# Sliding-window attention: two key blocks folded into one before the exponential, GpSimd work in short pieces, and the gate projection moved between units

## The chip, the cores and the metric

The kernel runs on one core of a Trainium2 chip. The metric is the device time of one execution in microseconds, taken as the median of several runs. A profiled execution of the same program gives the trace from which the rows below are quoted; its span runs from the first to the last instruction. Engines are named as the profile does: PE is TensorE (matmuls), PEld its weight loads, DVE is VectorE, ACT is ScalarE, POOL is GpSimd, and SP is the engine whose queue issues the DMAs.

## The reference

The input is a sequence of 2048 rows of 1024 floats. Two layers follow each other. The first is a gated retention layer in chunks of 128 rows; its code is not touched here. The second is a gated sliding-window attention: 16 query heads of 64 columns share 2 key/value heads, keys are looked at in blocks of 128, and each query sees its own position and the 127 before it, so it needs its own key block and the one before. A sink per head enters the softmax's denominator.

```python
q, gate = jnp.split(rmsnorm(x, g_norm) @ w_in, [SWA_Q_WIDTH], axis=-1)
q = rmsnorm(q.reshape(b, nb, BLOCK, SWA_KV_HEADS, SWA_GROUP, SWA_HEAD_DIM), g_q)
scores = jnp.einsum('bnqkgd,bnjkd->bnkgqj', q, k_band) * (SWA_HEAD_DIM ** -0.5) + bias
scores = jnp.where(mask, scores, -jnp.inf)      # 0 <= dist < 128, key position >= 0
m = jnp.maximum(jnp.max(scores, axis=-1, keepdims=True), sink)
p = jnp.exp(scores - m)
p = p / (jnp.sum(p, axis=-1, keepdims=True) + jnp.exp(sink - m))
o = jnp.einsum('bnkgqj,bnjkd->bnqkgd', p, v_band).reshape(b, s, SWA_Q_WIDTH)
return x + (o * jax.nn.silu(gate)) @ w_out
```

Of the 256 keys of the two blocks exactly 128 are in a query's window: query i sees key j of its own block where j <= i, and key j of the block before where j > i. At any column j one of the two scores is therefore masked.

## The kernel before, in words

All arithmetic is fp32. A large matmul is split: each operand becomes a high part (type fp32r) and a low part, the difference, and three matmuls are summed (lines 149 to 151 and 153 to 155 in `proj`). The high part of a weight tile is made on ScalarE (L127) and the low part by a subtraction (L129), on VectorE in the retention layer and in the first pass over a weight, on GpSimd otherwise. A projection covers 512 rows, takes four PSUM banks, loads its weight in tiles of 128 x 1024 and yields after each tile and after its evacuation.

The attention layer is `phase_b`. Its unit is one group of 512 rows (4 of them) and one key/value head (2), 8 units in all. For a unit u there are:

- `main(u)`: for the first head of a group the keys and values (`evac_kv`, which fills the key store `kst` and the values `vst`), then the queries (`evac_q`: copy out of PSUM to `qn`, squares, sum, reciprocal root on GpSimd at L107/L108, scaling, split into `qs` at L804/L805, transposes at L813, copies to `qst` at L817 and L819).
- `gates(u)`: the gate projection; `evac_g` applies tanh (L833) and forms the gate (L834).
- `attn(u)`: for each of the four row blocks m and each parity `par` of the heads (a half, four heads): score matmuls over two key blocks (L870), addition of the bias and running minimum of the negated score into P (L873), the sink's term (L879, L880), the exponential with its sum (L881), denominator (L883, L884), scaling (L887), transposes of P by block (L891), copies to SBUF (L895 on VectorE, L897 on ScalarE). Then the product with V (L907), the gate (L910) and the split into `ohi` and `olo` (L911, L912).
- `out_b(u)`: the output projection of a unit's `ohi` and `olo`, whose evacuation adds the residual `res` (loaded and stored at L924 to L926). `ohi` and `olo` have one buffer each, so `out_b(u-1)` must have read them before `attn(u)` writes them.
- `prep_b(u)`: calls `prep`, which loads the rows of the next group, scales them (L189), and splits them (L191, L192) into `xhi` and `xlo`. `stats` makes the scale `rb` from row sums. `out_last` is the output projection of the last unit, in halves (L959 to L962).

`filler(u)` strings the projections that run beside `attn(u)`: gates of u, output projection of u-1, `main` of u+1. `drive` emits them in turns, one step of the filler for each 0.6 steps spent on attention (1.0 in the first unit), and gives attention's instructions a priority 300 places ahead; a planner with a model of times then sets the order on each engine. `attn(u)` does not emit a product with V before the gates of u are emitted.

Of the kernel before, what the change touches and what calls it, by code (L numbers as in the profile page):

```python
# [36 lines left out]
PSUM_BUFS = {"rr": 4, "s": 2, "f": 2}  # L37
RAW = 3
# [20 lines left out]
def tile_yoco(ctx, tc, x, x_t, w_qk, w_vg, wo_a, w_kv, w_b, wo_b, ag, kvg, bg, kng, qng,  # L59
# [53 lines left out]
    def wload(src, cols, name, kscale=None, key=None):  # L113
# [14 lines left out]
        eng = nc.gpsimd if psum["phase"] == "b" and kscale is None else nc.vector  # L128
        eng.tensor_tensor(lo, raw, hi.bitcast(F32), op=ALU.subtract)  # L129
        return hi, lo  # L130

    def proj(src, nk, xhi, xlo, feat, evac, name, kscale=None, key=None, cols=512, before=None):
        kn = 1024 // cols
        bk = [pbank("ab"[m // 2], f"pp_{name}_{m}") for m in range(4)]
        for kp in range(nk // kn):
            if before is not None:
                before(kp)
            hi, lo = wload(src[kp], cols, f"{name}_{kp}",
                           None if kscale is None else kscale[:, kp * kn : (kp + 1) * kn], (key, kp))
# [43 lines left out]
    def prep(g, rb):  # L183

        xhi, xlo = xt_tiles(f"b{g}")
        for kp in range(KT // 2):
            raw = wp.tile([P, 2, T], F32, tag="raw", bufs=RAW, name=f"xraw_b{g}_{kp}")
            nc.sync.dma_start(raw, xmid[g][kp])
            nc.gpsimd.tensor_tensor(raw, raw, rb.unsqueeze(1).to_broadcast([P, 2, T]), op=ALU.mult)  # L189
# [539 lines left out]
    def phase_b(pb):  # L729
# [4 lines left out]
        kst = cst.tile([P, KVH * 2, 2 * MT + 1, P], F32R, name="kst")  # L734
        gq = cst.tile([P, HD], F32, name="gq")
# [15 lines left out]
        def main(u):  # L751
            g, kv = units[u]
            n = f"b{u}"
            if kv == 0:
# [4 lines left out]
                vst = p2.tile([P, MT, KVH * HD], F32, tag="vst", name=f"vst_{n}")  # L759
                st["kv", g] = vst  # L760

                def evac_kv(m, ps):
                    kr = p1.tile([P, 512], F32, tag="qn", bufs=2, name=f"kn_{n}_{m}")
                    nc.scalar.copy(kr[:, : 2 * KVH * HD], ps[:, : 2 * KVH * HD])
                    nc.vector.tensor_copy(vst[:, m, :], kr[:, KVH * HD : 2 * KVH * HD])
# [21 lines left out]
                    nc.vector.tensor_copy(kst[:, :, kb + m + 1, :], tp.rearrange("p (a t) -> p a t", a=4))  # L787
# [5 lines left out]
            def evac_q(m, ps):  # L793
                qn = p1.tile([P, 512], F32, tag="qn", bufs=2, name=f"qn_{n}_{m}")
# [12 lines left out]
                qT = p1.tile([P, GQ, P], F32R, tag="qst", bufs=6, name=f"qst_{n}_{m}")  # L807
                qst.append(qT)
                for half in range(2):
# [6 lines left out]
                    if half:  # L816
                        nc.scalar.copy(dst, t3)  # L817
                    else:
                        nc.vector.tensor_copy(dst, t3)  # L819
# [4 lines left out]
        def gates(u):  # L824
# [10 lines left out]

            yield from proj(w_b[kv, 1], KT, xhi, xlo, True, evac_g, f"{n}g", kscale=bgs, key=("g", kv))
            st["gate", u] = gate

        def attn(u):
# [7 lines left out]
            for m in range(MT):  # L847
# [11 lines left out]
                for par in range(2):  # L859
# [3 lines left out]
                    for j in range(4):  # L863
# [5 lines left out]
                        for hl in range(2):  # L869
# [6 lines left out]
                            op0=ALU.add, op1=ALU.min, accum_out=nm[:, c : c + 1])  # L876
                        if j == 3:
# [3 lines left out]
                        nc.scalar.activation(pt[:, j, :w], pt[:, j, :w], AF.Exp, scale=-1.0,  # L881
                                             bias=nm[:, c : c + 1], accum_out=den[:, c : c + 1])
                    nc.vector.tensor_tensor(den[:, hs], den[:, hs], es[:, hs], op=ALU.add)  # L883
                    nc.vector.reciprocal(den[:, hs], den[:, hs])  # L884
                    for j in range(4):
                        c = 4 * par + j
                        nc.vector.tensor_scalar_mul(pt[:, j, :w], pt[:, j, :w], den[:, c : c + 1])  # L887
# [205 lines left out]
```

## Time and profile before

| | us |
|---|---|
| median of 3 runs | 2522.36 (2522.0 to 2522.67) |
| profiled execution, whole time | 2513.12 |
| its span | 2511.3 |
| TensorE busy / weight loads busy | 2446.6 / 1995.4 |
| VectorE, ScalarE, GpSimd busy | 1714.5, 1128.1, 477.2 |
| granted TensorE clock, mean | 0.99 |

Rows of groups read: line, engine, operation, output <- inputs, shape, count | busy time, mean ns of one | idle time of the engine ahead of them and what ended it. Rows of waits read: waiting instruction <- what ended the wait: total us, times, longest. Rows of stretches give the stretch, its length, busy us and instruction count of each engine, granted clock, share of the DMA engines, GB/s. Rows of tiles give shortest/median/longest ns. Matmuls are pipelined, so the duration of one is longer than the distance to the next.

### The profile page before, as it was taken

Reading aid. Unit: us, or ns where it says so; the run is one execution under the profiler, and the core shown is the slowest. Engines: PE = TensorE matmul, PEld = TensorE weight load, DVE = VectorE, ACT = ScalarE, POOL = GpSimd, SP = SyncE. Lnnn points to the kernel's source line nnn. Section 1 sums busy time; section 2 is a strip of 40 time slices with the busy share of each in tenths; the row PEclk is TensorE's granted clock in tenths of the full one; section 3 lists DMA queues with packets and bytes.
Section 4 is the critical chain, followed back from the end, with each engine's and each line's share of the span. In section 5 each row is a group of like instructions: output and inputs, shape, how many; then the busy total and the mean of one; then the engine's idle time right before and its main releaser. Section 6 shows DMA issues by size and latency. Waiting matters only on the chain.

```text
span 2511.3 us, 32377 instructions
## 1 busy us (share of the span) xinstructions
PE 2446.6 (97%) x11816; PEld 1995.4 (79%) x11816; DVE 1714.5 (68%) x2953; ACT 1128.1 (45%) x2008; POOL 477.2 (19%) x393
## 2 busy tenths in 40 slices
PE   8999999999999999999999999989899999999998
PEld 6888787888888888888888888777677777777887
DVE  5546674786868657667666576677867677677766
ACT  4333233544436445435354354435544455445553
POOL 0000000021000020000010000042335444353360
PEclk9999999999999999999999999999899999999999
DMA  8434873586636455465364243374233342342432
GB/s 294 135 115 132 262 268 119 162 290 228 229 119 201 147 168 159 158 212 184 119 206 152 91 159 111 103 256 156 76 118 122 105 156 74 132 144 84 135 116 94
DMA packets 141035, 395.05 MB, mean 157 GB/s; under 512 B 16411, under 2 KB 28876, under 8 KB 140876
## 3 DMA queue, kind: packets, MB, share of 16 engines
q1 hardware_dynamic: 140876, 392.99, 47.3%
q8 instruction: 93, 1.52, 0.2%
q14 instruction: 66, 0.54, 0.1%
HBM read 321.60 MB, written 74.47 MB: 158 GB/s over the span
## 4 chain that ended last, share of the span: by engine, by line
PE 81%; DMA 8%; DVE 7%; ACT 2%; issue 1%; POOL 0%; SPq 0%; DVEq 0%; ACTq 0%
PE pp_ao L151 4%; PE pp_ao L149 4%; PE pp_ao L150 4%; PE o_t L907 2%; PE s_t L870 2%; PE pT_t L891 2%; PE pp_bo L149 1%; PE pp_bo L150 1%; PE pp_bo L151 1%; DMA res<-xmid 1%; PE ot_r L643 1%; PE dl_r L607 1%; PE o_r L615 1%; PE dl_r L608 1%; PE o_r L617 1%
## 5 line engine op out<-in xcount | busy, mean ns | idle before, releaser
L149 PE MATMUL pp_ao<-ohi_r,whi_ao 128*128 128x512 f32 x512 | 199.7, 394 | 4.9 <-DVE x_r L679 2.7
L150 PE MATMUL pp_ao<-olo_r,whi_ao 128*128 128x512 f32 x512 | 201.7, 394 | 0.0
L107 POOL TENSOR_SCALAR r_o_r<-sso_r,ep 128x1 f32<-128x1 f32 x48 | 28.6, 596 | 904.6 <-ACT jo_r L637 904.6
L881 ACT ACTIVATE P_t<-P_t,nm_t 128x256 f32<-128x256 f32 (+1 forms) x256 | 127.7, 499 | 157.3 <-DVE nm_t L873 156.7
L151 PE MATMUL pp_ao<-ohi_r,wlo_ao 128*128 128x512 f32 x512 | 196.7, 394 | 0.1
L873 DVE CUSTOM_DVE_ANT_0 P_t<-s_t,bias,nsnk 128x256 f32<-128x256 f32 (+1 forms) x256 | 116.5, 470 | 36.8 <-PE s_t L870 35.8
L127 ACT CAST whi_ao<-raw_ao 128x1024 fp32r<-128x1024 f32 x64 | 67.2, 1050 | 153.1 <-issue 47.5
L129 DVE TENSOR_TENSOR wlo_ao<-raw_ao,whi_ao 128x1024 fp32r<-128x1024 f32 x64 | 78.1, 1223 | 81.7 <-ACT whi_ao L127 80.3
L703 ACT CAST Shi_r<-S 128x512 fp32r<-128x512 f32 x120 | 69.9, 618 | 116.5 <-PE o_r L617 88.0
L149 PEld LDWEIGHTS pp_ao<-ohi_r,whi_ao 128*128 128x128 f32 x512 | 96.9, 189 | 26.0 <-DVE x_r L679 3.1
L151 PEld LDWEIGHTS pp_ao<-ohi_r,wlo_ao 128*128 128x128 f32 x512 | 97.1, 190 | 21.7 <-DVE wlo_ao L129 1.1
L150 PEld LDWEIGHTS pp_ao<-olo_r,whi_ao 128*128 128x128 f32 x512 | 97.4, 190 | 20.5 <-issue 0.2
L704 DVE TENSOR_TENSOR Slo_r<-S,Shi_r 128x512 fp32r<-128x512 f32 x120 | 85.4, 737 | 40.1 <-ACT Shi_r L703 39.9
L870 PE MATMUL s_t<-kst,qst_b 128*128 128x256 f32 (+1 forms) x512 | 103.3, 299 | 8.6 <-DVE nm_t L873 8.5
L870 PEld LDWEIGHTS s_t<-kst,qst_b 128*128 128x128 f32 x512 | 84.8, 193 | 30.8 <-DVE nm_t L873 11.5
L630 DVE SCALAR_TENSOR_TENSOR S<-S,dl_r 128x512 f32<-128x512 f32 x112 | 74.6, 682 | 41.4 <-PE dl_r L609 41.3
L887 DVE TENSOR_SCALAR P_t<-P_t,den_t 128x256 f32<-128x256 f32 (+1 forms) x256 | 95.0, 434 | 1.8
L679 DVE TENSOR_TENSOR x_r<-x_r,pp_ao 128x512 f32<-128x512 f32 x128 | 84.0, 683 | 14.1 <-PE pp_ao L151 14.0
L149 PE MATMUL pp_bo<-ohi_t,whi_bo 128*128 128x512 f32 x224 | 89.1, 406 | 1.3 <-DVE gate_b L834 1.1
L150 PE MATMUL pp_bo<-olo_t,whi_bo 128*128 128x512 f32 x224 | 89.0, 397 | 0.0
L129 POOL TENSOR_TENSOR wlo_bo<-raw_bo,whi_bo 128x1024 fp32r<-128x1024 f32 x28 | 70.5, 2523 | 93.9 <-ACT whi_bo L127 80.0
L151 PE MATMUL pp_bo<-ohi_t,wlo_bo 128*128 128x512 f32 x224 | 87.7, 396 | 0.0
(1037 smaller groups left out, 7464.1 us busy)
## 6 DMA issues: line engine op xcount, KB each, us to landing
raw_ao<-in_wo_a SPq DMA_DIRECT2D x64, 512.0 KB, 3.6
b<-in_w_vg SPq DMA_DIRECT2D x64, 256.0 KB, 5.1
res<-xmid SPq DMA_DIRECT2D x56, 256.0 KB, 3.0
raw_bo<-in_wo_b SPq DMA_DIRECT2D x28, 512.0 KB, 3.6
x_r<-in_x_t SPq DMA_DIRECT2D x16, 512.0 KB, 5.8
xin<-in_x SPq DMA_DIRECT2D x16, 512.0 KB, 3.5
xmid<-x_r SPq DMA_DIRECT2D x16, 512.0 KB, 4.3
xraw_b<-xmid SPq DMA_DIRECT2D x16, 512.0 KB, 3.6
```

What stands on the lines that cost most here:

```text
L129: eng.tensor_tensor(lo, raw, hi.bitcast(F32), op=ALU.subtract)
L149: nc.tensor.matmul(o, hi[:, kk, sl], xh, start=st, stop=False)
L150: nc.tensor.matmul(o, hi[:, kk, sl], xl, start=False, stop=False)
L151: nc.tensor.matmul(o, lo[:, kk, sl], xh, start=False, stop=sp)
L630: nc.vector.scalar_tensor_tensor(S32[:, d, :], S32[:, d, :], gamC[h], dl[d], op0=ALU.mult, op1=ALU.add)
L679: nc.vector.tensor_tensor(t, t, ps, op=ALU.add)
L703: nc.scalar.copy(hi, src[:, d, :])
L704: nc.vector.tensor_tensor(lo, src[:, d, :], hi.bitcast(F32), op=ALU.subtract)
L870: nc.tensor.matmul(o, qst[m][:, h, :], kst[:, kv * 2 + hl, kb + b0 : kb + 2, :], start=hl == 0, stop=hl == 1)
L873: nc.vector.tensor_tensor_reduce(out=pt[:, j, :w], in0=o, in1=bias[:, kv * GQ + h, b0 * P :], scale=-1.0, scalar=nsv[:, h : h + 1], op0=AL ...
L881: nc.scalar.activation(pt[:, j, :w], pt[:, j, :w], AF.Exp, scale=-1.0, bias=nm[:, c : c + 1], accum_out=den[:, c : c + 1])
L887: nc.vector.tensor_scalar_mul(pt[:, j, :w], pt[:, j, :w], den[:, c : c + 1])
```

## The change

In attention the two key blocks of a half are folded by a minimum after every second head, so that P has 128 columns a head from there on. The exponential, the scaling (one instruction for four heads, with a broadcast) and the transposes run on these. The transposed P is copied twice, once as it is (ScalarE) and once times a triangular mask (VectorE). The first copy is multiplied with the values of the block before, the second with the difference of own values and those before, which `evac_kv` now makes beside the values. The first row block of the sequence has one key block and no fold.

GpSimd's subtractions for low parts are cut into pieces of 256 columns, the scaling in `prep` goes from GpSimd to VectorE, and copies to `qst` and `kst` go from VectorE to ScalarE. `qn` has four buffers for two, `qst` seven for six. In `filler`, the gates of unit u+1 follow `main(u+1)`, so they are emitted beside attention of u; those of the last unit stay at the start of the last filler. The row statistics come behind the output projection.

```diff
--- before.py
+++ after.py
@@ -35,6 +35,8 @@
 PSUM_BUFS = {"rr": 4, "s": 2, "f": 2}
+PIECE = 256
+QN = 4
 RAW = 3
@@ -125,8 +127,14 @@
         nc.scalar.copy(hi, raw)
-        eng = nc.gpsimd if psum["phase"] == "b" and kscale is None else nc.vector
-        eng.tensor_tensor(lo, raw, hi.bitcast(F32), op=ALU.subtract)
+        if psum["phase"] == "b" and kscale is None:
+            for k in range(kn):
+                for c in range(0, cols, PIECE):
+                    t = (slice(None), k, slice(c, c + PIECE))
+                    nc.gpsimd.tensor_tensor(lo[t], raw[t], hi[t].bitcast(F32), op=ALU.subtract)
+        else:
+            nc.vector.tensor_tensor(lo, raw, hi.bitcast(F32), op=ALU.subtract)
         return hi, lo
@@ -186,7 +195,7 @@
             nc.sync.dma_start(raw, xmid[g][kp])
-            nc.gpsimd.tensor_tensor(raw, raw, rb.unsqueeze(1).to_broadcast([P, 2, T]), op=ALU.mult)
+            nc.vector.tensor_tensor(raw, raw, rb.unsqueeze(1).to_broadcast([P, 2, T]), op=ALU.mult)
             hi, lo = xhi[kp], xlo[kp]
@@ -732,6 +741,8 @@
         kst = cst.tile([P, KVH * 2, 2 * MT + 1, P], F32R, name="kst")
+        mask = cst.tile([P, P], F32, name="mask_b")
+        nc.sync.dma_start(mask, mask_t)
         gq = cst.tile([P, HD], F32, name="gq")
@@ -756,13 +767,18 @@
                     nc.gpsimd.tensor_copy(kst[:, :, 0, :], kst[:, :, 2 * MT, :].bitcast(F32))
-                vst = p2.tile([P, MT, KVH * HD], F32, tag="vst", name=f"vst_{n}")
+                vst = p2.tile([P, 2, MT, KVH * HD], F32, tag="vst", name=f"vst_{n}")
                 st["kv", g] = vst
                 def evac_kv(m, ps):
-                    kr = p1.tile([P, 512], F32, tag="qn", bufs=2, name=f"kn_{n}_{m}")
+                    kr = p1.tile([P, 512], F32, tag="qn", bufs=QN, name=f"kn_{n}_{m}")
                     nc.scalar.copy(kr[:, : 2 * KVH * HD], ps[:, : 2 * KVH * HD])
-                    nc.vector.tensor_copy(vst[:, m, :], kr[:, KVH * HD : 2 * KVH * HD])
+                    v = vst[:, 0, m, :]
+                    nc.vector.tensor_copy(v, kr[:, KVH * HD : 2 * KVH * HD])
+                    if g or m:
+                        before = (vst if m else st["kv", g - 1])[:, 0, (m - 1) % MT, :]
+                        nc.vector.tensor_tensor(vst[:, 1, m, :], v, before, op=ALU.subtract)
                     kr = kr[:, : KVH * HD]
@@ -784,14 +800,14 @@
                         nc.tensor.transpose(tr[:, j * P : (j + 1) * P], kd[:, j // 2, j % 2, :], ident_r)
-                    nc.vector.tensor_copy(kst[:, :, kb + m + 1, :], tp.rearrange("p (a t) -> p a t", a=4))
+                    nc.scalar.copy(kst[:, :, kb + m + 1, :], tp.rearrange("p (a t) -> p a t", a=4))
...
             def evac_q(m, ps):
-                qn = p1.tile([P, 512], F32, tag="qn", bufs=2, name=f"qn_{n}_{m}")
+                qn = p1.tile([P, 512], F32, tag="qn", bufs=QN, name=f"qn_{n}_{m}")
                 nc.scalar.copy(qn, ps)
@@ -804,7 +820,7 @@
                                         op=ALU.subtract)
-                qT = p1.tile([P, GQ, P], F32R, tag="qst", bufs=6, name=f"qst_{n}_{m}")
+                qT = p1.tile([P, GQ, P], F32R, tag="qst", bufs=7, name=f"qst_{n}_{m}")
                 qst.append(qT)
@@ -813,10 +829,7 @@
                     t3 = tp.rearrange("p (a t) -> p a t", a=4)
-                    if half:
-                        nc.scalar.copy(dst, t3)
-                    else:
-                        nc.vector.tensor_copy(dst, t3)
+                    nc.scalar.copy(dst, t3)
@@ -833,8 +846,9 @@
+            st["gate", u] = gate
             yield from proj(w_b[kv, 1], KT, xhi, xlo, True, evac_g, f"{n}g", kscale=bgs, key=("g", kv))
-            st["gate", u] = gate
+            st["gated", u] = True
@@ -874,35 +888,41 @@
                             op0=ALU.add, op1=ALU.min, accum_out=nm[:, c : c + 1])
+                        if j % 2 and nb == 2:
+                            pj = pt[:, j - 1 : j + 1, :]
+                            nc.vector.tensor_tensor(pj[:, :, :P], pj[:, :, :P], pj[:, :, P:], op=ALU.min)
                         if j == 3:
...
                             nc.scalar.activation(es[:, hs], es[:, hs], AF.Exp)
-                        nc.scalar.activation(pt[:, j, :w], pt[:, j, :w], AF.Exp, scale=-1.0,
+                    for j in range(4):
+                        c = 4 * par + j
+                        nc.scalar.activation(pt[:, j, :P], pt[:, j, :P], AF.Exp, scale=-1.0,
                                              bias=nm[:, c : c + 1], accum_out=den[:, c : c + 1])
                     nc.vector.reciprocal(den[:, hs], den[:, hs])
+                    pw = pt[:, :, :P]
+                    nc.vector.tensor_tensor(pw, pw, den[:, hs].unsqueeze(2).to_broadcast([P, 4, P]), op=ALU.mult)
+                    tp = bank(f"pT_{n}_{m}_{par}", "f")
                     for j in range(4):
-                        c = 4 * par + j
-                        nc.vector.tensor_scalar_mul(pt[:, j, :w], pt[:, j, :w], den[:, c : c + 1])
+                        nc.tensor.transpose(tp[:, j * P : (j + 1) * P], pt[:, j, :P], ident)
+                    t = [p2.tile([P, 512], F32, tag=f"pT{par}", name=f"pTs_{n}_{m}_{b}_{par}") for b in range(nb)]
+                    nc.scalar.copy(t[0], tp)
+                    if nb == 2:
+                        a4 = lambda x: x.rearrange("p (a t) -> p a t", a=4)
+                        nc.vector.tensor_tensor(a4(t[1]), a4(tp), mask.unsqueeze(1).to_broadcast([P, 4, P]),
+                                                op=ALU.mult)
                     for b in range(nb):
-                        tp = bank(f"pT_{n}_{m}_{b}_{par}", "f")
-                        for j in range(4):
-                            nc.tensor.transpose(tp[:, j * P : (j + 1) * P],
-                                                pt[:, j, b * P : (b + 1) * P], ident)
-                        t = p2.tile([P, 512], F32, tag=f"pT{par}", name=f"pTs_{n}_{m}_{b}_{par}")
-                        if b:
-                            nc.vector.tensor_copy(t, tp)
-                        else:
-                            nc.scalar.copy(t, tp)
-                        pT[b, par] = t
+                        pT[b, par] = t[b]
                     yield
-                while ("gate", u) not in st:
+                while ("gated", u) not in st:
                     yield
...
                     blk = m - 1 + b0 + b
-                    vv = (cur if blk >= 0 else prev)[:, blk % MT, kv * HD : (kv + 1) * HD]
+                    vv = (cur if blk >= 0 else prev)[:, 1 if b else 0, blk % MT, kv * HD : (kv + 1) * HD]
                     for par in range(2):
@@ -937,7 +957,10 @@
                     nc.scalar.copy(hi, raw)
-                    nc.gpsimd.tensor_tensor(lo, raw, hi.bitcast(F32), op=ALU.subtract)
+                    for k in range(2):
+                        for c in range(0, T, PIECE):
+                            t = (slice(None), k, slice(c, c + PIECE))
+                            nc.gpsimd.tensor_tensor(lo[t], raw[t], hi[t].bitcast(F32), op=ALU.subtract)
             yield
@@ -969,19 +992,23 @@
         def filler(u):
-            yield from gates(u)
-            if units[u][1] == 0 and u + 2 < nu:
-                t = [p1.tile([P, T], F32, tag=k, bufs=b, name=f"st{k}_{u}") for k, b in (("sq", 1), ("qn", 2))]
-                st["rb"] = stats(units[u][0] + 1, t, "f")
-            o = out_b(u - 1) if u > 0 else iter(())
-            if u + 1 < nu and units[u + 1][1] == 0:
+            o = out_b(u - 1) if u > 0 else gates(u)
+            if u + 1 == nu:
+                yield from gates(u)
+                yield from o
+                yield from out_last(u)
+                return
+            if units[u + 1][1] == 0:
                 for _ in prep_b(u + 1):
             yield from o
-            if u + 1 < nu:
-                yield from main(u + 1)
-            else:
-                yield from out_last(u)
+            if units[u][1] == 0 and u + 2 < nu:
+                t = [p1.tile([P, T], F32, tag=k, bufs=b, name=f"st{k}_{u}") for k, b in (("sq", 1), ("qn", QN))]
+                st["rb"] = stats(units[u][0] + 1, t, "f")
+            yield from main(u + 1)
+            if u + 2 < nu:
+                yield from gates(u + 1)
...
             pass
```

More of the change, by code (lines that the diff above doesn't have):

```diff
@@ L138, in proj @@
             hi, lo = wload(src[kp], cols, f"{name}_{kp}",
-                           None if kscale is None else kscale[:, kp * kn : (kp + 1) * kn], (key, kp))
+                           None if kscale is None else kscale[:, kp * kn : (kp + 1) * kn],
+                           (key, kp))
             for kk in range(kn):
```

## The prediction

> **What bounds the kernel now.** I read the page first, then busy times by stretch, then TensorE's waits in the attention layer.
>
> ```profile
> span 2511.3 us, 32377 instructions
> PE 2446.6 (97%) x11816; PEld 1995.4 (79%) x11816; DVE 1714.5 (68%) x2953; ACT 1128.1 (45%) x2008; POOL 477.2 (19%) x393
> ...
> PE 81%; DMA 8%; DVE 7%; ACT 2%; issue 1%; POOL 0%; SPq 0%; DVEq 0%; ACTq 0%
> ```
>
> TensorE is busy for 97% of the span and carries 81% of the chain that ended last, so work taken from it should come off the time, unless it lies where TensorE waits. The stretches show where that is. 1709 is where the first attention scores start; everything before it keeps its code except the four multiplications of `prep`.
>
> ```profile
> core 0: us, PE busy (x) PEld busy (x) DVE busy (x) ACT busy (x) POOL busy (x), PEclk, DMA share, GB/s
> 0.00:1709.00 1709.00, 1680.07 (x7699) 1388.97 (x7700) 1139.74 (x1512) 729.74 (x1044) 159.37 (x206) 0.99 0.54 177
> 1709.00:1782.30 73.30, 71.31 (x375) 57.38 (x373) 61.31 (x146) 42.26 (x97) 23.18 (x17) 1.00 0.39 127
> 1782.30:1812.60 30.30, 21.69 (x101) 13.89 (x101) 27.43 (x81) 17.85 (x53) 6.30 (x3) 0.72 0.24 85
> 1812.60:2458.00 645.40, 629.79 (x3338) 498.49 (x3339) 454.53 (x1112) 321.80 (x763) 288.38 (x168) 1.00 0.35 118
> 2458.00:2511.30 53.30, 43.77 (x309) 36.63 (x305) 31.53 (x105) 16.43 (x53) 0.00 (x0) 0.96 0.25 82
> ```
>
> The long stretch from 1812.6 to 2458 is TensorE's: 629.8 of 645.4 us, with VectorE at 454.5 (70%). The stretch 1782.3 to 1812.6 is a hole: gates of unit 1 are done, `out_b` of unit 0 cannot start before attention of unit 0 has ended, TensorE works 21.7 of 30.3 us at a clock of 0.72, and VectorE works 27.4, so VectorE sets its end. The last stretch is the tail of the last unit. TensorE's waits say the same:
>
> ```profile
> PE s_t L870 <- DVE nm_t L873: 8.5, 7, 3.2
> PE qtp_b L813 <- DVE qs_b L805: 6.6, 3, 3.1
> ...
> PE pp_b4g L149 <- ACT qn_b L795: 0.9, 1, 0.9
> ```
>
> **Part 1: transposes.** Before, each half (m, par) transposes P in two blocks of four; now the two blocks are folded by a minimum ahead of the exponential and only four are left. There are 64 halves, 4 of them with one block already.
>
> ```profile
> L891 PE MATMUL pT_t<-ident_r,P_t x496: 270/272/476, 1731.1 to 2491.3; 128*128 128x128 f32 x166
> ```
>
> From the timeline (start, time, engine, line):
>
> ```profile
> 1757.38 0.39 PE L151 MATMUL pp_b1g<-xhi_b,wlo_b1g 128*128 128x512 f32 x1
> 1757.62 1.03 PE L891 MATMUL pT_t<-ident_r,P_t 128*128 128x128 f32 x8
> 1758.41 0.48 PE L149 MATMUL pp_b1g<-xhi_b,whi_b1g 128*128 128x512 f32 x1
> 1758.72 0.40 PE L150 MATMUL pp_b1g<-xlo_b,whi_b1g 128*128 128x512 f32 x1
> ```
>
> 496 becomes 64 x 4 = 256, so 240 go. The 272 ns of one are pipelined and not its price. From start to start, eight transposes and the matmul behind them take 1758.72 - 1757.62 = 1.10 us; a 512-column matmul alone takes 1757.62 - 1757.38 = 0.24. Eight cost 0.86, one 0.107. 240 x 0.107 = 25.8 us of TensorE. Of unit 0, whose attention ends in the hole at VectorE's pace, 6 halves lose four each: 24 x 0.107 = 2.6 us do not count. **Term 1: -23.** The matmuls of scores and of P with V keep their number and shape, so nothing else leaves TensorE.
>
> **Part 2: GpSimd in pieces, `prep` on VectorE.** Tile rows give shortest, median and longest time of an instruction:
>
> ```profile
> L879 DVE TENSOR_TENSOR es_t<-snk,nm_t x64: 146/161/2298, 1720.5 to 2486.8; 128x4 f32<-128x4 f32 x64
> L887 DVE TENSOR_SCALAR P_t<-P_t,den_t x256: 279/349/2533, 1727.4 to 2489.6; 128x256 f32<-128x256 f32 x120, 128x128 f32<-128x128 f32 x8
> L895 DVE COPY pTs_t<-pT_t x60: 674/691/693, 1752.3 to 2491.6; 128x512 f32<-128x512 f32 x60
> L192 DVE TENSOR_TENSOR xlo_b<-xraw_b,xhi_b x16: 1210/2109/3024, 1640.0 to 2234.3; 128x1024 fp32r<-128x1024 f32 x16
> L129 POOL TENSOR_TENSOR wlo_bo<-raw_bo,whi_bo x28: 2377/2406/3384, 1773.0 to 2444.6; 128x1024 fp32r<-128x1024 f32 x28
> ```
>
> An addition of four columns that takes 161 ns sometimes takes 2298, about one GpSimd instruction (2406) long, while the copy out of PSUM never exceeds 693. VectorE instructions on SBUF operands are held while GpSimd runs. In the hole's beginning it stands in order of time (first two rows GpSimd, then VectorE, then TensorE with its idle time in brackets):
>
> ```profile
> 1775.49 2.80 POOL L189 TENSOR_TENSOR xraw_b<-xraw_b,rb 128x1024 f32<-128x1024 f32 x1
> 1778.54 2.41 POOL L129 TENSOR_TENSOR wlo_bo<-raw_bo,whi_bo 128x1024 fp32r<-128x1024 f32 x1 [0.24 <-ACT whi_bo L127]
> 1775.96 2.36 DVE L883 TENSOR_TENSOR den_t<-den_t,es_t 128x4 f32<-128x4 f32 x1
> 1778.56 5.44 DVE L887 TENSOR_SCALAR P_t<-P_t,den_t 128x256 f32<-128x256 f32 x4
> 1784.46 0.91 PE L870 MATMUL s_t<-kst,qst_b 128*128 128x256 f32 x4 [2.19 <-DVE nm_t L873]
> 1788.77 0.72 PE L813 MATMUL qtp_b<-ident_r,qs_b 128*128 128x128 f32 x4 [3.10 <-DVE qs_b L805]
> ```
>
> Here den_t, four columns like L879, lost 2.2 us, four scalings lost 5.44 - 4 x 0.349 = 4.0, and the `xlo_b` subtractions about 0.9 each over 1.21, two of them in the hole: about 8 us of VectorE time from 1775 to 1797. Between two GpSimd instructions VectorE got in (den_t ends at 1778.32, the next GpSimd instruction starts at 1778.54). A piece of 256 columns takes between 2406/4 = 0.60 and, where one carries a start cost of its own, some 0.8 us (my bound), so a hold should fall to a third.
>
> The Trainium skill, "GPSIMD Engine Reference", section Key points, says that GpSimd shares its SBUF interfaces with VectorE and contends with instructions in a two-port mode or with two SBUF inputs; the rows above agree. By that rule the change is only half a cure: the new minima and the one scaling have two SBUF inputs and stay exposed. This gives rival B below.
>
> `prep`'s multiplication moves to VectorE: 16 x 1.2 us (nearest row: 1.21, the shortest L192 of the same size) = 19 us, 4 in each group, so 4.9 in the hole's approach. Its GpSimd time (16 x 2.4) goes. The other prices:
>
> ```profile
> L819 DVE CAST qst_b<-qtp_b 128x512 fp32r<-128x512 f32 x32 | 21.9, 683 | 1.3 <-PE qtp_b L813 1.3
> L910 DVE TENSOR_TENSOR gate_b<-gate_b,o_t 128x512 f32<-128x512 f32 x32 | 21.9, 683 | 31.8 <-PE o_t L907 31.8
> ...
> L962 DVE TENSOR_TENSOR res_l<-res_l,pp_l 128x256 f32<-128x256 f32 x16 | 6.7, 420 | 9.5 <-PE pp_l L961 9.5
> ```
>
> ScalarE's groups:
>
> ```profile
> L881 ACT ACTIVATE P_t<-P_t,nm_t 128x256 f32<-128x256 f32 x240 | 121.4, 506 | 145.8 <-DVE nm_t L873 145.2
> ...
> L817 ACT CAST qst_b<-qtp_b 128x512 fp32r<-128x512 f32 x32 | 18.6, 582 | 5.5 <-PE qtp_b L813 5.4
> ...
> L881 ACT ACTIVATE P_t<-P_t,nm_t 128x128 f32<-128x128 f32 x16 | 6.3, 396 | 11.5 <-DVE nm_t L873 11.5
> ```
>
> **VectorE's account after 1709.** Added: 120 minima x 0.42 (L962, 256 elements) = 50; 64 scalings of 128x512 x 0.68 (L910) = 44; 15 differences of V, at most 0.42 each = 6; 12 of `prep`'s 16 x 1.2 = 14. Masked copies take the place of the plain ones at the same 0.69. Removed: 256 scalings x 0.349 = 89; 32 query copies x 0.683 = 22; 16 key copies of the same size = 11. Sum -8, then what GpSimd's holds give back. I take VectorE at 540 to 575 of some 770 us, hidden behind TensorE outside hole and tail. If that cover were gone, the 114 us added would show.
>
> The Trainium skill, "VectorE: DVE Perf Modes", section "Mode 2x_2P", puts fp32 scalings at two elements a cycle and two-tensor instructions at one. It speaks against this part, and rows agree: 256 elements cost 349 ns as a scaling and 420 in a two-tensor form. By the page's one element a cycle at 0.96 GHz plus 156 ns, an estimate of a minimum is 423 ns, which gives the same sum.
>
> **ScalarE:** 240 exponentials fall by 506 - 396 = 110 ns: -26 us; it takes over 48 copies of 0.58 us (L817): +28. At 398 of 802 us busy it hides this. **GpSimd:** three more starts in 86 splits, 0 to 0.2 us each: 0 to 52 us, less 29 of `prep` after 1709; it has 318 of 802 us. Behind it wait the splits' matmuls and SP's weight loads, which wait for `raw` to come free: up to 0.6 us later on 1024 rows, against three buffers.
>
> **Term 2, the hole.** VectorE there and in its approach: 8 us of holds, of which I count three quarters as gone (-6), `prep` +4.9, four query copies -2.7, smaller holds before 1775 -3 (an allowance). Sum -7. Ends: 0 (GpSimd's pieces hold as long) and -15 (21.7 us at clock 0.72 is 15.6 at full clock; 30.3 - 15.6). **Term 2: -7.**
>
> **Term 3, query chain.** `qn` gets four buffers for two and GpSimd no longer holds the chain for 2.4 us: of qs_b's remaining 3.5 us (6.6 less 3.1 in the hole) and the 0.9 waits for qn_b, 5.3 with b6g's equal one, I count -4 (ends 0 and -5). TensorE's other waits stay: nothing ahead of them is touched.
>
> **Part 4, order of the fillers.** The chain of projections stays gates(u), out_b(u-1), main(u+1), gates(u+1), both before and after; what moves is that attention of u is put beside out_b(u-1), main(u+1), gates(u+1) and no longer beside gates(u). All their DMAs keep their order on SP, except the row statistics (one load, ahead of main). Attention's last step moves some 1.2 filler steps later but has main and gates before out_b(u) needs it. 0, ends -5 (waits left over) and +88 (rival A).
>
> **Sum:** -23 - 7 - 4 = -34 us, from the profiled execution's 2513.1 to 2479. The median of the runs shown is 2522.4, 9.2 above that execution; by the same difference, **2488**.
>
> **Rivals.**
> A, slower: attention of each unit ends too late and out_b(u) opens with a hole like the first. One costs 30.3 - 15.6 = 14.7 us; six more cost 88, less 34: 2576. From the third added hole it is slower than before. For it: attention starts later beside the fillers. Against: after 1812.6 TensorE idles only 15.6 us in 645, and gates(u+1) now lies in between. 8%.
> B: four pieces run back to back and hold VectorE as long as one did. Terms 2 and 3 vanish: 2522 - 23 = 2499; with `prep`'s 4.9 us showing in the hole, 2504. For it: pieces have no wait between them. Against: VectorE got in between two GpSimd instructions above. 15%.
> C: attention's latency and not TensorE sets the pace, the transposes' time turns into idle time: 2522. The 97% speak against it. 5%.
> D: the hole closes and TensorE's idle 35.7 us after 1709 mostly go: -23 - 15 - 20: 2464. 5%.
> My forecast, between -20 and -50: 67%.
>
> **Chances.** Faster 0.87 (forecast, B, D), within 0.2% (5 us, about what a measurement of this kernel can tell from no change) 0.05 (C), slower 0.08. The range 2467 to 2510 leaves out A, C and most of D, 0.18.
>
> **What would show it.** 256 transposes; a clock near 1.00 after 1782 and a shorter hole; longest L879 under 1 us; no wait of qtp for qs_b over 1 us. Wrong if TensorE's idle time after 1709 exceeds 36 us, above all ahead of `pp_bo`.

## The result, and the profile after

| | before | after |
|---|---|---|
| median (range), us | 2522.18 (2519.37 to 2522.67) | 2532.68 (2531.13 to 2535.77) |
| ratio to before | | 1.0043, 95% interval 1.0028 to 1.0059 |
| profiled execution, us | 2513.12 | 2535.77 |

The changed kernel is slower by 0.43%; 2488 was forecast. The profiled execution of before was a quick one of its kind, so the two traces differ by 22.6 us where the medians differ by 10.5. The traces serve for where the time went, the medians for how much. The head of the page after:

```profile
span 2533.9 us, 32159 instructions
PE 2465.3 (97%) x11576; PEld 1980.9 (78%) x11576; DVE 1659.4 (65%) x2864; ACT 1121.9 (44%) x2056; POOL 502.5 (20%) x635
```

240 matmuls fewer, as intended, and TensorE is busy 18.7 us longer. The stretch behind the first attention scores, of before and then of after (columns as in the prediction's stretches):

```profile
1709.00:2511.30 802.30, 766.56 (x4119) 606.39 (x4117) 574.79 (x1442) 398.35 (x965) 317.86 (x187) 0.98 0.35 115
```

```profile
1709.00:2533.90 824.90, 789.24 (x3893) 596.37 (x3891) 524.57 (x1356) 391.84 (x1012) 355.28 (x436) 0.97 0.35 112
```

In these stretches all 22.6 us are TensorE's busy time (766.6 to 789.2): its idle time is 35.7 us in both. Not all of it is the change's. The last matmul of the retention layer (`pp_ao`), whose code is the same, starts at 1649.9 before and at 1654.1 after, so some 4 us arose ahead of the attention layer, and behind 1709 they show as projections still to be done. VectorE became 50 us lighter. So no wait took the place of another; some matmuls became dearer. Groups show which. First before, then after (busy us, mean ns | idle ahead of them):

```profile
L870 PE MATMUL s_t<-kst,qst_b 128*128 128x256 f32 (+1 forms) x512 | 103.3, 299 | 8.6 <-DVE nm_t L873 8.5
L891 PE MATMUL pT_t<-ident_r,P_t 128*128 128x128 f32 x496 | 78.2, 281 | 1.0 <-ACT qst_b L817 0.4 <-ACT pTs_t L897 0.3 <-DVE P_t L887 0.2
L907 PE MATMUL o_t<-pTs_t,vst_b 128*64 128x512 f32 x248 | 68.4, 618 | 2.2 <-ACT pTs_t L897 2.2
```

```profile
L884 PE MATMUL s_t<-kst,qst_b 128*128 128x256 f32 (+1 forms) x512 | 104.9, 305 | 12.2 <-DVE nm_t L887 12.0
L927 PE MATMUL o_t<-pTs_t,vst_b 128*64 128x512 f32 x248 | 98.7, 630 | 1.0 <-DVE pTs_t L915 0.7 <-ACT pTs_t L911 0.4
L909 PE MATMUL pT_t<-ident_r,P_t 128*128 128x128 f32 x256 | 45.4, 290 | 10.2 <-DVE P_t L906 9.6 <-ACT qst_b L832 0.6
```

The product of P with V: the same 248 records of the same shape and nearly the same mean duration, but 30.3 us more of TensorE's time. A busy time counts overlap once, so the records overlap less than before. The timeline shows it. A row groups neighbouring records; one of these fp32 matmuls with 64 output columns leaves two records, so x8 is the four matmuls of a row block (two key blocks times two halves of heads; the halves write columns 0 to 63 and 64 to 127). Before:

```profile
1943.29 1.94 PE L907 MATMUL o_t<-pTs_t,vst_b 128*64 128x512 f32 x8
1945.15 0.50 PE L149 MATMUL pp_bo<-ohi_t,whi_bo 128*128 128x512 f32 x1
```

After, the same place:

```profile
1942.92 1.07 PE L927 MATMUL o_t<-pTs_t,vst_b 128*64 128x512 f32 x2
1943.92 0.50 PE L159 MATMUL pp_bo<-olo_t,whi_bo 128*128 128x512 f32 x1
...
1947.80 1.08 PE L927 MATMUL o_t<-pTs_t,vst_b 128*64 128x512 f32 x4
1948.81 0.50 PE L158 MATMUL pp_bo<-ohi_t,whi_bo 128*128 128x512 f32 x1
1949.15 0.40 PE L159 MATMUL pp_bo<-olo_t,whi_bo 128*128 128x512 f32 x1
1949.48 1.07 PE L927 MATMUL o_t<-pTs_t,vst_b 128*64 128x512 f32 x2
1950.48 0.50 PE L160 MATMUL pp_bo<-ohi_t,wlo_bo 128*128 128x512 f32 x1
```

From start to start a pair takes 1948.81 - 1947.80 = 1.01 us and a lone matmul 1943.92 - 1942.92 = 1.00, the same. Four together take 1.86; here they take 1.00 + 1.01 + 1.00 = 3.01. Call PV records with no other matmul between them a streak. Before has 38 streaks, 25 of them of x8 and 7 of a lone x2; after has 84, 2 of x8 and 53 of a lone x2. Summing over the timeline from 1700 on the distance from each row to the next, idle time left out: PV 65.9 to 93.1 us, transposes 49.7 to 30.2, scores 71.0 to 78.6, projections 558.1 to 563.6. That is +27 - 20 + 8 + 6 = +21 of the 22.7; most of the projections' 6 are the 4 us from ahead of the attention layer.

### The profile page after: what moved, and what is told of

Read it like the earlier page. It is cut to its first block, busy times and chain, and to the rows that moved or that the text cites. A ratio compares the mean times of both kernels' runs of the same rounds, so it can differ in the third digit from the quotient of the medians.

```text
span 2533.9 us, 32159 instructions
## 1 busy us (share of the span) xinstructions
PE 2465.3 (97%) x11576; PEld 1980.9 (78%) x11576; DVE 1659.4 (65%) x2864; ACT 1121.9 (44%) x2056; POOL 502.5 (20%) x635
## 5 line engine op out<-in xcount | busy, mean ns | idle before, releaser
L158 PE MATMUL pp_ao<-ohi_r,whi_ao 128*128 128x512 f32 x512 | 199.6, 394 | 7.3 <-ACT gate_a L427 3.3
L159 PE MATMUL pp_ao<-olo_r,whi_ao 128*128 128x512 f32 x512 | 201.1, 393 | 0.0
L901 ACT ACTIVATE P_t<-P_t,nm_t 128x128 f32<-128x128 f32 x256 | 100.9, 395 | 129.1 <-DVE P_t L894 116.7
L129 ACT CAST whi_ao<-raw_ao 128x1024 fp32r<-128x1024 f32 x64 | 67.2, 1050 | 155.0 <-issue 46.9
L712 ACT CAST Shi_r<-S 128x512 fp32r<-128x512 f32 x120 | 69.9, 618 | 115.3 <-PE o_r L626 88.0
L158 PEld LDWEIGHTS pp_ao<-ohi_r,whi_ao 128*128 128x128 f32 x512 | 96.9, 189 | 28.8 <-ACT gate_a L427 3.7
L135 POOL TENSOR_TENSOR wlo_bo<-raw_bo,whi_bo 128x256 fp32r<-128x256 f32 x112 | 94.2, 873 | 102.1 <-ACT whi_bo L129 74.5
L159 PEld LDWEIGHTS pp_ao<-olo_r,whi_ao 128*128 128x128 f32 x512 | 97.0, 189 | 20.4 <-issue 0.2
L713 DVE TENSOR_TENSOR Slo_r<-S,Shi_r 128x512 fp32r<-128x512 f32 x120 | 85.3, 736 | 39.0 <-ACT Shi_r L712 38.8
L927 PE MATMUL o_t<-pTs_t,vst_b 128*64 128x512 f32 x248 | 98.7, 630 | 1.0 <-DVE pTs_t L915 0.7
L158 PE MATMUL pp_bo<-ohi_t,whi_bo 128*128 128x512 f32 x224 | 88.6, 401 | 2.1 <-DVE gate_b L847 1.5
L159 PE MATMUL pp_bo<-olo_t,whi_bo 128*128 128x512 f32 x224 | 88.8, 397 | 0.0
```

Of the source, the lines that this page charges most:

```text
L135: nc.gpsimd.tensor_tensor(lo[t], raw[t], hi[t].bitcast(F32), op=ALU.subtract)
L158: nc.tensor.matmul(o, hi[:, kk, sl], xh, start=st, stop=False)
L159: nc.tensor.matmul(o, hi[:, kk, sl], xl, start=False, stop=False)
L713: nc.vector.tensor_tensor(lo, src[:, d, :], hi.bitcast(F32), op=ALU.subtract)
L901: nc.scalar.activation(pt[:, j, :P], pt[:, j, :P], AF.Exp, scale=-1.0, bias=nm[:, c : c + 1], accum_out=den[:, c : c + 1])
L927: nc.tensor.matmul(op[par * HD : (par + 1) * HD, :], vv, pT[b, par], start=b == 0, stop=b == nb - 1)
```

## The experiments

Theory: the halves' PV matmuls run at the same time on two halves of TensorE's columns when they stand together; the changed program's order tears them apart, and that costs some 30 us. Rivals: the filler order (rival A's subject), the fold's longer chain on VectorE, or a cost of each change between 64 and 128 columns. All times in us. PV is the busy time of its TensorE group, idle is TensorE's idle time from 1709 to the end; both are of the profiled execution. Before ran at 2519.5 to 2519.9 beside these.

| kernel | median (range) | ratio to before | PV | idle |
|---|---|---|---|---|
| before | 2522.18 | | 68.4 | 35.7 |
| after | 2532.68 | 1.0043 (1.0028 to 1.0059) | 98.7 | 35.7 |
| e1_pairs | 2503.71 (2500.65 to 2505.37) | 0.9940 (0.9923 to 0.9956) | 67.1 | 39.1 |
| e2_split | 2523.46 (2516.97 to 2529.41) | 1.0016 (1.0002 to 1.0030) | 68.5 | 38.8 |
| e3_old_fillers | 2534.07 (2533.73 to 2538.75) | 1.0061 (1.0044 to 1.0078) | 100.3 | 41.3 |
| e4_fold_only | 2547.69 (2544.76 to 2549.47) | 1.0114 (1.0098 to 1.0130) | 98.0 | 51.1 |
| e5_pairs_old_fillers | 2503.06 (2501.41 to 2505.32) | 0.9934 (0.9919 to 0.9949) | 69.9 | 46.9 |
| e6_pairs_whole | 2518.28 (2514.85 to 2524.36) | 0.9996 (0.9986 to 1.0005) | 67.6 | 50.2 |
| e7_before_pieces | 2516.61 (2509.43 to 2522.90) | 0.9988 (0.9976 to 1.0000) | 69.8 | 36.5 |
| e8_two_banks | 2510.87 (2505.83 to 2521.03) | 0.9963 (0.9950 to 0.9976) | 80.1 | 38.0 |
| e9_halves | 2504.35 (2504.10 to 2505.71) | 0.9947 (0.9929 to 0.9965) | 63.8 | 46.9 |
| e10_same_half | 2544.97 (2539.53 to 2545.39) | 1.0100 (1.0076 to 1.0124) | 117.5 | 37.9 |
| e11_banks_pairs | 2508.31 (2503.27 to 2513.94) | 0.9959 (0.9945 to 0.9973) | 69.5 | 41.2 |
| e12_pieces_pairs | 2508.75 (2502.20 to 2511.90) | 0.9956 (0.9942 to 0.9970) | 64.5 | 32.1 |

### e1_pairs: after, with PV kept together

```diff
+                last = None
...
-                    for par in range(2):
-                        nc.tensor.matmul(op[par * HD : (par + 1) * HD, :], vv, pT[b, par],
-                                         start=b == 0, stop=b == nb - 1)
+                    for par in (1, 0):
+                        mm = lambda: nc.tensor.matmul(op[par * HD : (par + 1) * HD, :], vv, pT[b, par],
+                                                      start=b == 0, stop=b == nb - 1)
+                        if last is None:
+                            last = mm()
+                        else:
+                            with tc.issue_after(last.ins):
+                                last = mm()
```

The half that is ready last comes first, and each matmul is placed behind the one before it.

> The changed kernel with one edit: of the four matmuls of P with V per row block, the two that write the upper and the lower 64 PSUM partitions are issued next to each other. Theory T1 (two such matmuls run at the same time when adjacent, about 0.96 us for both, while one alone takes 1.0; the change broke up 25 to 30 of these pairs): 58 lone ones become 29 pairs, 90 -> 60 us of TensorE, so 26 to 30 us faster than the changed kernel, about 2505. Rival T2 (the later place of attention beside the fillers and the clock dips cause the loss): within 5 us of the changed kernel, about 2530. Rival T3 (VectorE's longer chain is the bound): same as T2.

```profile
L928 PE MATMUL o_t<-pTs_t,vst_b 128*64 128x512 f32 x248 | 67.1, 630 | 1.6 <-ACT pTs_t L911 1.4
```

PV is back at 67.1 us, and the time falls by 29.0 us (2532.68 to 2503.71), below before. The edit fixes the order of 124 matmuls and leaves every instruction as it is; the planner then places others differently around them.

### e2_split: before, PV half by half

e1's chain in the kernel before, with the two key blocks of the first half ahead of those of the second.

> The kernel before with one edit: the four matmuls of P with V go half by half (both key blocks of the upper 64 partitions, then both of the lower), so only the middle two can form a pair. T1: three steps of about 1 us for each row block where there were two, some 62 lone matmuls instead of 12: 22 to 28 us slower, about 2547. T2, T3: nothing changes on VectorE and in the order of units: 2522 +- 3.

```profile
1946.75 1.94 PE L908 MATMUL o_t<-pTs_t,vst_b 128*64 128x512 f32 x8
1948.63 0.74 PE L870 MATMUL s_t<-kst,qst_b 128*128 128x256 f32 x4
```

A miss for me: four matmuls take 1.88 us in this order too, and the kernel is hardly slower (1.0016, 1.0002 to 1.0030). Order inside an undisturbed streak doesn't matter; what matters is that no full-width matmul stands in it.

### e3_old_fillers and e5_pairs_old_fillers: the filler order

```diff
-            o = out_b(u - 1) if u > 0 else gates(u)
-            if u + 1 == nu:
...
+            yield from gates(u)
...
+            o = out_b(u - 1) if u > 0 else iter(())
...
-            if u + 2 < nu:
-                yield from gates(u + 1)
+            if u + 1 < nu:
+                yield from main(u + 1)
```

`filler` and the gate's flag as before (so the row statistics too are ahead of the output projection again), in after (e3) and in e1 (e5).

> The changed kernel with the fillers in the old order (gates of u beside attention of u); fold, pieces, copies and buffers as changed. T1: the matmuls of P with V stay broken up (the planner puts 56 alone, 58 in the changed kernel), so within 5 us of the changed kernel, 2527 to 2537. T2: the loss goes, 2500 or less.

> The changed kernel with the matmuls of P with V kept together (as in e1_pairs) and the fillers in the old order. If the new place of the gates is worth nothing, as the prediction had it: 2504 +- 5, like e1_pairs. If it causes the new waits after unit 2's and unit 4's queries (2.8 and 2.9 us each at a lower clock): 8 to 12 us faster than e1_pairs, about 2494. If it helps: slower than 2510.

2534.07 against after's 2532.68, and 2503.06 against e1's 2503.71: the filler order is worth less than 1.5 us in either, and it did not tear PV apart (PV 100.3 with the old order).

### e4_fold_only and e6_pairs_whole: without the GpSimd part

```diff
-            for k in range(kn):
-                for c in range(0, cols, PIECE):
...
+        eng = nc.gpsimd if psum["phase"] == "b" and kscale is None else nc.vector
+        eng.tensor_tensor(lo, raw, hi.bitcast(F32), op=ALU.subtract)
...
-            nc.vector.tensor_tensor(raw, raw, rb.unsqueeze(1).to_broadcast([P, 2, T]), op=ALU.mult)
+            nc.gpsimd.tensor_tensor(raw, raw, rb.unsqueeze(1).to_broadcast([P, 2, T]), op=ALU.mult)
```

e4 is e3 with this edit (fold, copies and buffers alone), e6 is e1 with it.

> Fold, the copies moved to ScalarE and the larger buffers alone: GpSimd's subtractions whole, the scaling in prep on GpSimd, fillers in the old order. T1: -20 us of transposes and +24 of broken pairs, so near the kernel before, 2520 to 2535. If the pieces and prep on VectorE are what costs (T3), 2500; if GpSimd's holds on VectorE matter, it is slower than the variant with old fillers and pieces by 5 to 10 us.

> e1_pairs with GpSimd's subtractions whole and the scaling in prep on GpSimd again; fold, copies, buffers and new fillers stay. Theory of the prediction (GpSimd holds VectorE, terms 2 and 3): 8 to 14 us slower than e1_pairs, 2512 to 2518. Rival (holds are hidden behind TensorE, prep on VectorE costs as much as it saves): 2504 +- 4.

The fold with its copies and buffers, without the GpSimd part, tears PV apart (98.0 us) and makes the kernel slower by 1.1%. That is a miss: 2547.69 lies 13 us above the range expected. With the GpSimd part it is 13.6 us faster (e3 against e4, where 5 to 10 were expected), and 14.6 with PV together (e1 against e6, at the upper end of what was expected). What the short pieces relieve above all is TensorE's wait for the scaled P, in e4 and then in e3 (total, times, longest):

```profile
PE pT_t L902 <- DVE P_t L899: 17.1, 10, 5.2
```

```profile
PE pT_t L908 <- DVE P_t L905: 8.4, 4, 6.4
```

### e7_before_pieces and e12_pieces_pairs: without the fold

e7 is the kernel before with the opposite of e4's edit; e12 adds e1's edit.

> The kernel before with only GpSimd's subtractions in pieces of 256 and the scaling in prep on VectorE. Prediction's terms 2 and 3: 7 to 11 us faster than before, about 2510. Rival (holds hidden): 2520 +- 4.

> The kernel before with GpSimd in pieces of 256, prep on VectorE, and PV kept together, without fold: what the fold is worth is this time less that of e1_pairs. Theory: e7_before_pieces (2516.6) less what its 6 split pairs cost (PV 67.3 to some 63 us): 2512 (2508 to 2516), so the fold is worth 8 us of the 20 that its transposes save. Rival (the fold gives all it saves on TensorE): 2524. Other rival (the fold is worth nothing): 2504.

Alone the pieces are worth some 3 us (interval up to no gain), where 7 to 11 were expected: a miss, within the rival's range. e12 took 2508.75, in the range expected. On top of it the fold, with its copies, buffers and fillers, brings 5 us (e1: 2503.71) where its transposes save 24; e12's expectation was 8. The ranges of e12 and e1 overlap, and the profiled executions took 2502.20 us (e12) and 2505.37 (e1), so these two traces show where the gain goes and not the 5 us. Both stretches behind 1709, e12 and then e1:

```profile
1709.00:2500.30 791.30, 759.20 (x4123) 603.86 (x4121) 537.29 (x1455) 398.97 (x966) 341.17 (x434) 0.99 0.35 117
```

```profile
1709.00:2503.10 794.10, 755.03 (x3880) 590.94 (x3878) 523.81 (x1352) 388.25 (x1008) 355.06 (x433) 0.96 0.36 116
```

In these two executions 243 matmul records fewer take only 4.2 us off TensorE's busy time, idle time rises from 32.1 to 39.1, and the granted clock falls from 0.99 to 0.96. Start to start as above: transposes 50.5 to 26.3, but scores 70.4 to 78.2 and projections 553.2 to 564.2. Of TensorE's waits for VectorE those of the scores rise most, in e12 and then in e1; those for the scaled P go from 6.7 to 8.8 us.

```profile
PE s_t L877 <- DVE nm_t L880: 4.1, 6, 1.5
```

```profile
PE s_t L884 <- DVE nm_t L887: 13.5, 17, 1.8
```

A place in e1 where time is lost, at the end of the attention of a unit (start, time, engine, line; idle in brackets; VectorE and ScalarE merged in order of start):

```profile
1980.43 0.50 PE L884 MATMUL s_t<-kst,qst_b 128*128 128x256 f32 x2 [0.39 <-DVE nm_t L887]
...
1981.71 0.47 DVE L887 CUSTOM_DVE_ANT_0 P_t<-s_t,bias,nsnk 128x256 f32<-128x256 f32 x1
...
1982.20 0.65 DVE L938 SCALAR_TENSOR_TENSOR olo_t<-gate_b,ohi_t 128x512 fp32r<-128x512 f32 x1
...
1982.78 0.41 DVE L894 TENSOR_TENSOR P_t<-P_t 128x256 f32<-128x256 f32 x1
...
1983.19 0.68 DVE L906 TENSOR_TENSOR P_t<-P_t,den_t 128x512 f32<-128x512 f32 x1
...
1983.22 0.40 ACT L901 ACTIVATE P_t<-P_t,nm_t 128x128 f32<-128x128 f32 x1 [0.41 <-DVE P_t L894]
...
1984.01 0.63 PE L909 MATMUL pT_t<-ident_r,P_t 128*128 128x128 f32 x4 [3.08 <-DVE P_t L906]
...
1985.48 1.08 PE L909 MATMUL pT_t<-ident_r,P_t 128*128 128x128 f32 x4 [0.84 <-DVE P_t L906]
```

TensorE waits 3.08 and 0.84 us for the scaled P (L906). The fold (L894) stands between the scores and the exponential, and the scaling, before four instructions of one head each, is one of four heads that ends for all at once. The clock follows in the stretches there:

```profile
1980.00:1990.00 10.00, 5.70 (x25) 4.88 (x24) 6.74 (x22) 6.12 (x19) 1.21 (x2) 0.77 0.17 54
1990.00:2000.00 10.00, 10.00 (x37) 6.45 (x37) 7.61 (x14) 3.62 (x6) 6.50 (x6) 0.89 0.00 0
1986.00:1992.00 6.00, 6.00 (x21) 5.13 (x20) 2.49 (x8) 3.20 (x6) 1.90 (x4) 0.50 0.00 0
```

From 1986 to 1992 TensorE is never idle and has half its clock: two matmuls of the gate projection start 0.43 us apart there (1988.92 and 1989.35), for 0.23 at 1992.53 and 1992.76. So here 4 us of waiting are followed by 6 us in which every matmul is dearer. No run took the chain apart, so which of its two links costs more stays open; that the longer chain is what lowers the clock is read from this place and not tested. The Trainium skill, "TensorE: Matmul & The Clock Gate", section "HAM oscillation — how this bites in real kernels", has as its rule that TensorE should have no idle gap above some 3.4 us. Here neither gap is that long, and the clock fell to 0.77 and, right behind them, to 0.50: two shorter gaps close together stood ahead of it.

### e8_two_banks and e11_banks_pairs: why the order changed

```diff
-                    tp = bank(f"pT_{n}_{m}_{par}", "f")
+                    tps = [bank(f"pT_{n}_{m}_{par}_{i}", "f") for i in range(2)]
...
-                    nc.scalar.copy(t[0], tp)
+                    for i in range(2):
+                        nc.scalar.copy(t[0][:, 256 * i : 256 * i + 256], tps[i][:, :256])
```

A half's four transposes go to two PSUM banks, two heads each, as before the change a half also took two banks of the ring `f` (one for each key block); the copies on both engines are halved. e8 is after with this, e11 is e1 with it.

> The changed kernel, but the four transposes of a half go to two PSUM banks (two heads each), with two copies of 256 columns for one of 512 on each engine. T1 with its cause (the planner issued the matmuls of P with V alone because the fold halves the PSUM banks a half takes, so that the output bank comes free before the second half is ready): the planner now leaves 24 alone where it left 58, so 15 to 18 us faster than the changed kernel, 2515 to 2520, less up to 5 us for the added copies. If the banks have no part in it: 2530 or more.

> e1_pairs and e8_two_banks together: PV kept together, transposes of a half in two PSUM banks with two copies each. Theory (what e8_two_banks gained was PV staying together more often, 50 of 62 pairs for 33): nothing comes on top of e1_pairs, 2504 (2500 to 2509). Rival (the second bank lets attention run ahead by itself: e8 gained 22 us, of which only 16 stand in the PV account): 2498.

In the traces the two halves of a key block start together in 56 of 62 cases before, 33 after, 32 in e3 and e4, 46 in e8, and 62 in e1 (the 50 that an expectation gives for e8 is the program's order). e8 gets 13 of the 29 torn pairs back and is 22 us faster, 4 to 9 more than expected; 18.6 of the 22 stand in PV (98.7 to 80.1), and the rest is not accounted for. My reading: the fold halved the banks that a half takes from a ring of two; `op`, from the same ring, comes free earlier, and the planner issues the first half's products before the second half is ready. That e11 (2508.31) is no faster than e1 (2503.71) says that the banks helped through the pairs.

### e9_halves and e10_same_half: two column halves at a time, or dear changes of shape

e9 keeps the four together half by half; e10 is e9 with all four on the same 64 columns, so half of the heads are missing from its attention output.

```diff
-                        mm = lambda: nc.tensor.matmul(op[par * HD : (par + 1) * HD, :], vv, pT[b, par],
+                        mm = lambda: nc.tensor.matmul(op[:HD, :], vv, pT[b, par],
...
-                nc.vector.tensor_tensor(og, og, op.rearrange("p (a t) -> p a t", a=4), op=ALU.mult)
+                nc.vector.tensor_tensor(og[:HD], og[:HD], op[:HD].rearrange("p (a t) -> p a t", a=4), op=ALU.mult)
```

> The kernel after, with the four PV matmuls of a row block kept together, in another order than in e1_pairs: both blocks of the second half of heads, then both of the first half (columns 64 to 127 twice, then 0 to 63 twice). Theory (matmuls on different column halves run at the same time, also when they are not neighbours, as long as no full-width matmul comes between): a row block takes 1.95 us as in e2_split, PV about 30 x 1.95 + 2 x 1.03 = 61 us, time 2504 (2499 to 2509), as e1_pairs. Rival (only neighbouring matmuls on different halves overlap: here only the middle two could): 30 x 2.9 = 87 us, time about 2530.

> e9_halves with all four PV matmuls of a row block writing the same 64 columns (the second half of heads is computed and overwritten, and the gate multiplies only 64 of 128 partitions, so the attention output is incomplete). Same matmuls, same order, same neighbours, same number of changes between 64 and 128 columns. Theory (two column halves at the same time): nothing is left to overlap, a row block takes 4 x 0.95 = 3.8 us instead of 1.95, 30 x 1.85 = +55 us, time about 2559 (2545 to 2570). Rival (the kernel after paid for each change between a 64-column and a full-width matmul, whatever the half): as e9_halves, 2504.

Timeline of e9, then of e10:

```profile
1933.94 1.94 PE L928 MATMUL o_t<-pTs_t,vst_b 128*64 128x512 f32 x8
1935.81 0.50 PE L158 MATMUL pp_bo<-ohi_t,whi_bo 128*128 128x512 f32 x1
```

```profile
1968.14 3.65 PE L928 MATMUL o_t<-pTs_t,vst_b 128*64 128x512 f32 x8
1971.72 0.50 PE L884 MATMUL s_t<-kst,qst_b 128*128 128x256 f32 x2
```

1.87 us become 3.58, PV goes from 63.8 to 117.5 us, and the kernel from 2504.35 to 2544.97. Both have 32 streaks of PV, so the number of changes of shape is the same: what is lost here is that the halves run at the same time. The time rose by 41 us, just short of the range expected, and not by the 54 of PV: idle time shrank by 9.0 (46.9 to 37.9), and other matmuls took some 5 us less. The three lengths fit 0.16 us for a streak plus 0.85 for each matmul of the half that has more of them: 1.01, 1.86, 3.56.

A change of shape is not free either. In the rows of after shown above, the full-width matmul behind a streak (L158 at 1948.81) takes 0.34 us to the next start and the one ahead of a streak (L159 at 1949.15) 0.33, for 0.24 between two full-width ones in the prediction's rows. After has 84 streaks where e1 has 55. At 0.16 us for a streak and 0.2 for its two neighbours, up to 10 of the 29 us between them (an estimate) are paid for the number of streaks; I put the rest down to halves that no longer run at the same time. No experiment separates the two.

The Trainium skill, "TensorEngine Tiling (Array Packing)", section "Key Properties", says that tiles work independently, and that a change of tiling mode drains the array. The trace agrees with the first (1.01 us for two halves, 1.00 for one); what the second costs can lie in the 0.16 us and in the 0.1 us on either side of a streak, and no run shows how much of them it is.

## Why the prediction was wrong, point by point

- **The step that failed** is the last sentence of part 1: "The matmuls of scores and of P with V keep their number and shape, so nothing else leaves TensorE." P with V kept both and cost 27 us more (the scores 8, for which no run shows a cause), since its price hangs on its neighbours. I priced the eight transposes from start to start but took PV as given; 1.94 us for x8 against 1.07 for x2 stood in the trace of before. With PV together (e1) the sign is the one forecast: -16, the upper part of the range given (2503.7 in 2467 to 2510). That is partly luck: step by step the pieces bring 3 (e7), PV kept together 8 (e12), which the prediction did not have, and the fold 5.
- **Term 1 (-23)**: 256 transposes as foreseen, and their account fell by 20 us in the trace after. What it brought to the time is some 5 us (e12 to e1). In those two traces the rest went into 7 us of waits and into dearer scores and projections, at a clock of 0.96 for 0.99. I put it down to the fold's longer chain, which the prediction took for hidden (read from one place, not tested): "Sum -8, then what GpSimd's holds give back" was an account of VectorE's total, not of the chain through it.
- **Part 2** was right in its mechanism. VectorE's short instruction L897 (L879 before) shows it in its shortest, median and longest time:

```profile
L897 DVE TENSOR_TENSOR es_t<-snk,nm_t x64: 147/155/702, 1726.1 to 2503.6; 128x4 f32<-128x4 f32 x64
L135 POOL TENSOR_TENSOR wlo_bo<-raw_bo,whi_bo x112: 725/741/1776, 1774.8 to 2457.4; 128x256 fp32r<-128x256 f32 x112
```

  The longest fell from 2298 to 702 ns, about one piece (741), below the bound of 1 us given; rival B is refuted. VectorE's 524.6 us lie below the 540 to 575 forecast. What the pieces bring depends on the fold: 3 us without it (e7), 14 with it, where terms 2 and 3 had 11.
- **Term 2 (-7) did not come.** The stretch from the end of gates of unit 1 to `out_b` of unit 0, after:

```profile
1790.60:1819.90 29.30, 23.10 (x99) 13.69 (x97) 24.10 (x83) 19.01 (x63) 3.77 (x4) 0.77 0.22 72
```

  29.3 us for 30.3, clock 0.77 for 0.72. VectorE's 24.1 for 27.4 us shows that the holds went, and it no longer sets the end. In the chain that ended last there, P with V now has the largest share (24.6%, 14.0 before), where before VectorE's scalings (18.9%) and `xlo_b` (15.9%) led. Without the fold the pieces do shorten this stretch: from the last gate matmul to the first `pp_bo` it is 30.7 us before, 25.0 in e7 and 22.4 in e12. With the fold it is 29.3 in after and also in e1, so torn PV is not the reason; over all runs with the fold it is 25 to 36, and what holds it open is not settled.
- **Term 3 (-4)** was right where it stood and lost elsewhere: waits of qtp for qs_b fell from 6.6 to 0.8 us. "TensorE's other waits stay" was wrong:

```profile
PE s_t L884 <- DVE nm_t L887: 12.0, 15, 2.7
PE pT_t L909 <- DVE P_t L906: 9.6, 6, 2.9
...
PE qtp_b L829 <- DVE qs_b L821: 0.8, 2, 0.5
```

  The second was 0.2 us before (L891's row above).
- **Part 4 (0)** was right: e3 and e5. Rival A had the right sign for a wrong reason: `pp_bo` waits 1.9 us in all (1.5 and 0.4), not 14.7 a unit. Rival C, attention's latency, which I gave 5%, had the transposes' time turn into idle time; once PV is repaired, idle time takes 7 of the 24 us that they save (e12 to e1), and dearer scores and projections take more.
- My sign for being wrong, idle time above 36 us, did not appear: 35.7. A check on idle time alone misses work that gets dearer.

## What to carry to other kernels

A matmul that fills half of TensorE's columns cost next to nothing here beside its partner on the other half (1.01 us for both) and its full time alone (1.00): keep partners together by an explicit order, and look at their group's busy time after any edit near them, even one that only frees a buffer. Before an instruction is fused on another engine, ask whether its result is now ready later for the first consumer; a lighter engine total says nothing about a longer chain. The version that beats both kernels here is the change with PV kept together (e1, 2503.71 us; the old filler order does as well, 2503.06).

## What the runs showed of the hardware that I had not expected

- Matmuls on different column halves overlap also when they are not neighbours in the order (e2 and e9: 1.88 and 1.87 us for two of one half followed by two of the other), but not across a full-width matmul between them (after: 3.01 us in three separate rows).
- A GpSimd subtraction of 256 columns takes 741 ns where a quarter of the 1024-column one would be 602 (2406 / 4), so each piece costs some 0.14 us more; TensorE's waits after 1709 name no GpSimd instruction.
